# A hybrid diffusion step: five half tiles of the dense experts stay in PSUM, one bank rotates, and the finish is reordered

## The chip, the cores and the metric

One core of one Trainium2 chip runs the whole kernel. The metric is the device time of an execution in microseconds; the median of several is what is compared.

## The reference, cut to what matters

One layer for 256 context tokens and 1024 latent tokens, model width 1024: modulation, windowed attention and RG-LRU into one output projection, then PEER, which picks 16 of 16384 experts for each of 8 heads and each token, and a last norm. The change touches the end of the first half and PEER:

```python
o_att = attend(q, k, v, attn_sink)
o_rnn, hf, hb = rglru_mixer(xr, yg, rg_w_a, rg_b_a, rg_w_i, rg_b_i, rg_lambda, h0_f, h0_b)
mix = jnp.concatenate([o_att, o_rnn.astype(o_att.dtype)], axis=-1)
x = x + ga1 * jnp.einsum('bsm,md->bsd', mix, w_out)
h2 = modulated_norm(x, g_ffn, sh2, sc2)
x = x + ga2 * peer(h2, pq, psk, pu, pv)
...
u = jnp.take(u_tab, eid, axis=0)
act = jax.nn.gelu(jnp.einsum('td,thkd->thk', xb, u).astype(jnp.float32))
vv = jnp.take(v_tab, eid, axis=0)
return jnp.einsum('thk,thkd->td', (g * act).astype(vv.dtype), vv)
```

## The kernel before

Tokens go in tiles of 128: two context tiles and eight latent tiles. The stages run in this order: modulation, the context tiles' first half, latent projection and recurrence (lproj), latent attention (lattend), the latent finish (fin), retrieval of the expert numbers (ret, `choose`), `spread` with the early experts, and `dense`.

PEER is done in two ways. Six latent tiles are **dense**: each of the 16384 experts is applied to them, in 128 steps of 128 experts. A step multiplies the expert rows `u` with the tiles' activations (48 matmuls of 384 columns, in `experts_in`), applies gelu, multiplies with the tokens' expert weights (`gt`) and adds the product with the rows `v` to the tiles' sums. 44 of the 128 steps have their first part done earlier, in the stage early, and fetch it from DRAM (`ad`). The two context tiles and the last two latent tiles are **gathered** (`mix`): for each of 128 picks a row of `u` and a row of `v` come by an indirect DMA from GpSimd's queue (L859, L873), and VectorE forms one dot product (L862) or one scaled sum (L879). That is 4 x 256 = 1024 gathers. They are written between other work: `tick` adds a mark's microseconds to a count and lets the next gather out whenever the count reaches the step of the stage; the gathers of dense are also ordered behind the instruction that marked them (`paced`).

Products are made as three matmuls of split operands (`mm3`, L138 to L140): a high and a low part of each side.

In `dense`, experts go in rounds of two (`GROUP`). `add` makes a round's products: six tiles of two halves of 512 columns, 12 halves, each the sum of 6 matmuls. `N_RES` tiles (two, so four halves, `res`) keep their sums in PSUM over all rounds. The other eight halves rotate through two banks (`rot`): ScalarE evicts each to `q` (L764), and VectorE adds it to `acc` in SBUF (L765). The resident products are written first, then the rotating ones.

`finish` for the latent tiles does, tile by tile, 32 matmuls of the output projection (two halves, L526), two VectorE steps a half (L528, L529), the squares (L535), rstd on VectorE and GpSimd (`rstd_of`, L145 to L151), the scaling (L537), eight transposes with their copies (`to_columns`, L248, L255), a split (L134, L135), for the gathered tiles another set of transposes (L545), and at last a mark of 14 us. `final` makes the last norm of a tile and stores it.

The instructions of all engines come from a compiler that orders each engine's queue by priority (the written order) and by what is ready in its own model; so an instruction can stand ahead of one written before it, unless a dependence forbids it.

## Time and profile before

| | us |
|---|---|
| median of 3 runs | 3565.87 |
| lowest and highest | 3563.97, 3566.43 |
| the profiled execution | 3568.34 |
| its span, first to last instruction | 3566.5 |
| TensorE busy in the span | 3210.4 |
| VectorE busy | 3111.0 |
| GpSimd busy | 1716.4 |
| ScalarE busy | 1429.9 |

Busy times are of that one execution. PE is TensorE's matmuls, PEld its weight loads, DVE is VectorE, ACT is ScalarE, POOL is GpSimd, SP is the queue of most DMAs. A matmul's duration in the timeline runs to a modelled end, so products that follow each other closely overlap: the distance of two starts is what one costs. PEclk is the granted clock of TensorE, 1.00 being 2.4 GHz. A wait is put down to the releaser that came last.

### The profile page before, as it was taken

How to read it: one execution, taken by the hardware profiler on the slowest of the kernel's cores; microseconds unless marked ns; L12 is line 12 of the kernel's file. 1: busy time of each engine (PE TensorE's matmuls, PEld its weight loads, DVE VectorE, ACT ScalarE, POOL GpSimd, SP SyncE). 2: the span in 40 equal slices, each digit the busy share in tenths (PEclk: the TensorE clock that was granted, in tenths of full speed). 3: DMA queues.
4: the chain of work that ended last, by engine and by line, in shares of the span. 5: the costliest groups of instructions: out<-in, count | busy, mean ns of one | idle time of the engine just before them, and what ended most of it. 6: DMA issues, size and time to landing. Idle time of an engine off the chain costs nothing.

```text
span 3566.5 us, 48580 instructions
## 1 busy us (share of the span) xinstructions
PE 3210.4 (90%) x16982; PEld 2704.1 (76%) x16982; DVE 3111.0 (87%) x6762; ACT 1429.9 (40%) x2242; POOL 1716.4 (48%) x1146
## 2 busy tenths in 40 slices
PE   7788868777999888888899999999999999999994
PEld 4477645433889877778788888878888887888884
DVE  4649989877999999993599999989999998999998
ACT  5734647523112344433333334333334333333432
POOL 0012451466521223443266666656666655666665
PEclk9799989988999999999999999999999999999997
DMA  8342652588621367795699999989999998999996
GB/s 331 136 152 82 216 206 83 185 276 290 219 89 31 122 199 214 233 315 185 242 325 337 337 330 334 340 308 335 329 328 339 327 340 290 332 327 336 335 339 223
DMA packets 349141, 918.19 MB, mean 257 GB/s; under 512 B 29144, under 2 KB 150104, under 8 KB 345824
## 3 DMA queue, kind: packets, MB, share of 16 engines
q0 software_dynamic: 147456, 536.94, 42.9%
q1 hardware_dynamic: 201440, 378.16, 30.8%
q8 instruction: 133, 2.18, 0.2%
q14 instruction: 112, 0.92, 0.1%
HBM read 834.48 MB, written 80.50 MB: 257 GB/s over the span
## 4 chain that ended last, share of the span: by engine, by line
PE 43%; DVE 22%; issue 8%; DMA 8%; POOL 3%; ACT 2%; SPq 0%; POOLq 0%; DVEq 0%; ACTq 0%
PE u L138 6%; PE u L140 6%; PE u L139 6%; PE rot L138 5%; PE rot L140 5%; PE rot L139 5%; DVE acc L879 3%; DVE row L862 3%; DMA row<-in_peer_u,eid 2%; PE res L138 2%; PE res L139 2%; PE res L140 2%; DMA row<-in_peer_v,eid 2%; DMA ad<-a 2%; DVE oh L699 1%
## 5 line engine op out<-in xcount | busy, mean ns | idle before, releaser
L859 POOL DMA_INDIRECT row<-in_peer_u,eid x512 | 749.9, 1465 | 603.3 <-DVE acc L879 201.7
L873 POOL DMA_INDIRECT row<-in_peer_v,eid x512 | 719.9, 1406 | 583.6 <-DVE acc L879 283.7
L138 PE MATMUL u<-hh,uh 128*128 128x384 f32 x2048 | 707.1, 345 | 22.4 <-ACT a L1028 22.4
L140 PE MATMUL u<-hh,ul 128*128 128x384 f32 x2048 | 705.6, 345 | 4.7 <-DVE ul L135 4.7
L139 PE MATMUL u<-hl,uh 128*128 128x384 f32 x2048 | 707.1, 345 | 0.0
L879 DVE SCALAR_TENSOR_TENSOR acc<-row,w,acc 128x1024 f32<-128x1024 f32 x508 | 663.4, 1306 | 25.2 <-DMA row<-in_peer_v,eid 23.7
L862 DVE SCALAR_TENSOR_TENSOR row<-row,h 128x1024 f32<-128x1024 f32 x512 | 623.0, 1232 | 62.8 <-DMA row<-in_peer_u,eid 62.6
L764 ACT ACTIVATE q<-rot 128x512 f32<-128x512 f32 x504 | 300.0, 597 | 523.5 <-PE rot L140 295.5
L138 PE MATMUL rot<-vh,ah 128*128 128x512 f32 x1024 | 409.1, 400 | 16.6 <-ACT q L764 16.1
L138 PEld LDWEIGHTS u<-hh,uh 128*128 128x128 f32 x2048 | 394.7, 193 | 29.8 <-ACT a L1028 23.8
L140 PEld LDWEIGHTS u<-hh,ul 128*128 128x128 f32 x2048 | 394.2, 192 | 9.7 <-DVE ul L135 5.1
L139 PE MATMUL rot<-vl,ah 128*128 128x512 f32 x1024 | 401.4, 392 | 0.0
L140 PE MATMUL rot<-vh,al 128*128 128x512 f32 x1024 | 400.6, 392 | 0.0
L139 PEld LDWEIGHTS u<-hl,uh 128*128 128x128 f32 x2048 | 394.6, 193 | 4.5
L765 DVE TENSOR_TENSOR acc<-q,acc 128x512 f32<-128x512 f32 x504 | 341.8, 686 | 45.4 <-ACT q L764 42.3
L140 PE MATMUL mm<-hh,wl 128*128 128x256 f32 (+2 forms) x848 | 289.7, 342 | 9.8 <-POOL wl L135 6.9
L138 PE MATMUL mm<-hh,wh 128*128 128x256 f32 (+2 forms) x848 | 286.3, 338 | 5.6 <-ACT wh L134 5.6
L139 PE MATMUL mm<-hl,wh 128*128 128x256 f32 (+2 forms) x848 | 284.3, 335 | 0.0
L134 ACT ACTIVATE uh<-u 128x1024 fp32r<-128x1024 f32 x128 | 135.8, 1061 | 331.3 <-PE u L139 302.0
L135 POOL TENSOR_TENSOR ul<-u,uh 128x1024 fp32r<-128x1024 f32 x44 | 122.8, 2791 | 277.8 <-ACT uh L134 237.5
L138 PEld LDWEIGHTS rot<-vh,ah 128*128 128x128 f32 x1024 | 193.4, 189 | 74.9 <-ACT q L764 36.7
L140 PEld LDWEIGHTS rot<-vh,al 128*128 128x128 f32 x1024 | 193.2, 189 | 41.5
(271 smaller groups left out, 5955.3 us busy)
## 6 DMA issues: line engine op xcount, KB each, us to landing
u<-in_ut SPq DMA_DIRECT2D x128, 512.0 KB
v<-in_peer_v SPq DMA_DIRECT2D x128, 512.0 KB
gd<-stg SPq DMA_DIRECT2D x12, 4096.0 KB
gt<-gd SPq DMA_DIRECT2D x64, 768.0 KB
w<-in_w_mod SPq DMA_DIRECT2D x24, 1024.0 KB
ad<-a SPq DMA_DIRECT2D x88, 192.0 KB
a<-ad SPq DMA_DIRECT2D x44, 384.0 KB
w<-in_w_query SPq DMA_DIRECT2D x32, 512.0 KB
```

The costliest lines, as they stand in the source:

```text
L134: A.activation(hi, src, AF.Copy)
L135: return (eng or V).tensor_tensor(lo, src, hi, op=OP.subtract)
L138: T.matmul(out, lhs[0], rhs[0], start=first, stop=False)
L139: T.matmul(out, lhs[0], rhs[1], start=False, stop=False)
L140: T.matmul(out, lhs[1], rhs[0], start=False, stop=last)
L699: V.tensor_tensor(oh.rearrange(four, j=2), o2.rearrange(four, j=2), pairs(gh, ts), op=OP.mult)
L764: A.activation(q, p, AF.Copy)
L765: tick(share / (2 * (N_DENSE - N_RES)), V.tensor_tensor(y, q, y, op=OP.add))
L859: G.indirect_dma_start(out=u, out_offset=None, in_=i["peer_u"], in_offset=bass.IndirectOffsetOnAxis(ap=eid[:, k:k + 1], axis=0))
L862: V.scalar_tensor_tensor(u, u, 1.0, h2, op0=OP.mult, op1=OP.mult, accum_out=act[:, j:j + 1])
L873: G.indirect_dma_start(out=v, out_offset=None, in_=i["peer_v"], in_offset=bass.IndirectOffsetOnAxis(ap=eid[:, k:k + 1], axis=0))
L879: V.scalar_tensor_tensor(acc, v, w[:, j:j + 1], acc, op0=OP.mult, op1=OP.add)
```

## The change

Four things change.

- `dense`: `N_RES` counts halves now, five of them, in five banks; one bank rotates in place of two. `add` writes one rotating product, then one resident product, and so on; after five such pairs the last two rotating products follow each other. Seven halves a round are evicted and added. In the tail, `final` takes tile 2's first half from PSUM and its second from `acc`.
- `D_STEP` goes from 2.05 to 2.0: a gather for every 2.0 us of marks in dense.
- `finish` of the latent tiles: the norm of a tile (`normed`) is written after the next tile's matmuls, its transposes are queued behind the last of them (`issue_after`), and the marks are 3 after each half and 2 after a tile in place of 14. `x` has three buffers, `f` two.
- `final`: one multiplication in place of two runs on GpSimd.

```diff
-N_RES = 2
+N_RES = 5
-D_STEP = 2.05
+D_STEP = 2.0
@@ finish
+        def normed(t, x, behind):
+            ss = wk.tile([P, 1], F32, name="ss", bufs=2)
+            f = wk.tile([P, KD, P], F32, name="f", bufs=2)
+            A.activation(f.rearrange("p k t -> p (k t)"), x, AF.Square, accum_out=ss)
+            rs = rstd_of(ss, wk)
+            A.activation(x, x, AF.Copy, scale=rs)
+            hh, hl, us = dest(t)
+            with tc.issue_after(behind) if behind else nullcontext():
+                to_columns(ps, f, x, hh, hl, us, a2, b2, cond)
...
+        waiting = None
...
-                    x = wk.tile([P, D], F32, name="x", bufs=2)
+                    x = wk.tile([P, D], F32, name="x", bufs=3 if lat else 2)
...
-                        T.matmul(p, oT, wo[c0][:, k, wc], start=(k == 0), stop=(k == KD - 1))
+                        ins = T.matmul(p, oT, wo[c0][:, k, wc], start=(k == 0), stop=(k == KD - 1))
...
+                    if lat:
+                        tick(3)
...
-                to_columns(ps, f, x, hh, hl, us, a2, b2, cond)
...
-                tick(14)
+                if not lat:
+                    normed(t, x, None)
+                    tick(14)
+                    continue
+                if waiting:
+                    normed(*waiting, ins.ins)
+                waiting = t, x
+                tick(2)
+        if waiting:
+            normed(*waiting, None)
@@ dense
-            res = [[ps.tile([P, 512], F32, name=f"res{x}{hf}") for hf in range(2)] for x in range(N_RES)]
+            res = [ps.tile([P, 512], F32, name=f"res{r}") for r in range(N_RES)]
-            acc = [st.tile([P, D], F32, name=f"acc{x}") for x in range(N_RES, N_DENSE)]
+            acc = {x: st.tile([P, D], F32, name=f"acc{x}") for x in range(N_RES // 2, N_DENSE)}
@@ add
-                for it in group:
-                    for x in range(N_RES):
-                        for hf in range(2):
-                            product(res[x][hf], x, hf, it, 0, P - 1)
-                for x in range(N_RES, N_DENSE):
-                    for hf in range(2):
-                        p = ps.tile([P, 512], F32, name="rot", bufs=2)
+                stay = iter(range(N_RES))
+                for r in range(N_RES, 2 * N_DENSE):
+                    x, hf = divmod(r, 2)
+                    p = ps.tile([P, 512], F32, name="rot")
+                    for it in group:
+                        product(p, x, hf, it, c0, c0 + GROUP - 1)
+                    y = acc[x][:, hf * 512:(hf + 1) * 512]
+                    if c0 == 0:
+                        A.activation(y, p, AF.Copy)
+                    else:
+                        q = wk.tile([P, 512], F32, name="q", bufs=2)
+                        A.activation(q, p, AF.Copy)
+                        tick(share / (2 * N_DENSE - N_RES), V.tensor_tensor(y, q, y, op=OP.add))
+                    for s in stay:
                         for it in group:
-                            product(p, x, hf, it, c0, c0 + GROUP - 1)
...
+                            product(res[s], *divmod(s, 2), it, 0, P - 1)
+                        break
@@ final
-        (G if N_CTX + N_RES <= t < N_CTX + N_DENSE and t % 2 == 0 else V).tensor_tensor(y, y, ga2, op=OP.mult)
+        (G if N_CTX + N_RES // 2 < t < N_CTX + N_DENSE and t % 2 == 0 else V).tensor_tensor(y, y, ga2, op=OP.mult)
```

## Rows read from the trace of the kernel before

**Rows 1.** The page's totals: busy us (share of span) x instructions.
```profile
PE 3210.4 (90%) x16982; PEld 2704.1 (76%) x16982; DVE 3111.0 (87%) x6762; ACT 1429.9 (40%) x2242; POOL 1716.4 (48%) x1146
```
**Rows 2.** Busy us by stage: PE, PEld, DVE, ACT, POOL; then clock, DMA share, GB/s.
```profile
706.00:888.00 182.00, 134.22 (x348) 65.70 (x348) 132.88 (x198) 54.60 (x105) 115.64 (x90) 0.86 0.84 282
...
1420.00:1640.00 220.00, 187.48 (x1466) 168.09 (x1465) 205.58 (x441) 86.87 (x108) 89.06 (x50) 0.94 0.87 274
1640.00:1720.00 80.00, 67.84 (x360) 65.70 (x361) 15.83 (x48) 20.34 (x29) 16.62 (x9) 0.90 0.47 160
1720.00:3521.00 1801.00, 1774.69 (x8617) 1565.08 (x8615) 1679.20 (x2158) 687.38 (x1043) 1138.97 (x770) 0.99 0.90 326
3521.00:3566.50 45.50, 0.38 (x2) 0.00 (x0) 39.44 (x57) 11.04 (x20) 15.65 (x10) 0.55 0.39 149
```
**Rows 3.** Timeline of TensorE in dense: start us, us, engine, line, operation.
```profile
1902.57 0.39 PE L138 MATMUL rot<-vh,ah 128*128 128x512 f32 x1
1913.45 0.34 PE L138 MATMUL u<-hh,uh 128*128 128x384 f32 x1
1930.10 0.39 PE L138 MATMUL res<-vh,ah 128*128 128x512 f32 x1
```
**Rows 4.** Timeline of the finish: TensorE, and one row of ScalarE.
```profile
761.95 1.10 PE L248 MATMUL tr<-ident,x 128*128 128x128 f32 x8 [1.90 <-ACT x L537]
...
768.90 3.60 PE L526 MATMUL mm<-w,gy 128*128 128x512 f32 x8
772.33 3.60 PE L526 MATMUL mm<-w,qT 128*128 128x512 f32 x8
773.72 1.06 ACT L535 ACTIVATE f<-x 128x1024 f32<-128x1024 f32 x1 [7.07 <-DVE x L529]
781.52 1.97 PE L248 MATMUL tr<-ident,x 128*128 128x128 f32 x8 [5.59 <-ACT x L537]
...
880.03 1.97 PE L248 MATMUL tr<-ident,x 128*128 128x128 f32 x8 [17.89 <-ACT x L537]
```
**Rows 5.** Waits in the finish: us in total, times, longest us.
```profile
PE tr L248 <- ACT x L537: 46.2, 8, 17.9
```
**Rows 6.** Groups of VectorE in the finish; the last by min/median/max ns.
```profile
L862 DVE SCALAR_TENSOR_TENSOR row<-row,h 128x1024 f32<-128x1024 f32 x43 | 54.3, 1268 | 28.2 <-DMA row<-in_peer_u,eid 28.0
L879 DVE SCALAR_TENSOR_TENSOR acc<-row,w,acc 128x1024 f32<-128x1024 f32 x38 | 48.8, 1284 | 16.2 <-DMA row<-in_peer_v,eid 15.6
...
L528 DVE TENSOR_TENSOR y<-mm,ga x16: 678/682/692, 719.0 to 866.0; 128x512 f32<-128x512 f32 x16
```
**Rows 7.** Gathers issued ahead of the finish: ns min/median/max, first and last start.
```profile
L859 POOL DMA_INDIRECT row<-in_peer_u,eid x48: 937/1149/2744, 364.6 to 670.9; - x48
L873 POOL DMA_INDIRECT row<-in_peer_v,eid x46: 937/1000/2816, 404.1 to 703.8; - x46
```
**Rows 8.** Busy time of the finish's matmuls alone up to 862; columns as rows 2.
```profile
706.00:862.00 156.00, 116.73 (x256) 0.90 0.83 279
```
**Rows 9.** Timeline in dense: a product's last matmul and its eviction.
```profile
1903.71 0.39 PE L140 MATMUL rot<-vh,al 128*128 128x512 f32 x1
...
1904.13 0.60 ACT L764 ACTIVATE q<-rot 128x512 f32<-128x512 f32 x1 [2.94 <-PE rot L140]
```
**Rows 10.** The page's costliest groups: busy us, mean ns, idle before.
```profile
L765 DVE TENSOR_TENSOR acc<-q,acc 128x512 f32<-128x512 f32 x504 | 341.8, 686 | 45.4 <-ACT q L764 42.3
```
**Rows 11.** Waits of TensorE in dense, columns as rows 5.
```profile
PE rot L138 <- ACT q L764: 10.7, 7, 3.3
```
**Rows 12.** Timeline of TensorE in a round without expert products.
```profile
1958.82 0.39 PE L138 MATMUL rot<-vh,ah 128*128 128x512 f32 x1
1959.05 0.39 PE L138 MATMUL res<-vh,ah 128*128 128x512 f32 x1
```
**Rows 13.** Timeline of the tail.
```profile
3528.11 3.40 DVE L837 TENSOR_TENSOR row<-row,vh 128x1024 f32<-128x1024 f32 x1 [0.77 <-DMA vh<-modd]
```
**Rows 14.** Busy time in one stretch of dense, columns as rows 2.
```profile
2900.00:3000.00 100.00, 89.76 (x406) 78.29 (x405) 88.62 (x114) 33.17 (x51) 62.42 (x43) 0.93 0.90 324
```

## What the change was predicted to do

> **What bounds the kernel now.** I read the page's engine totals first, then the busy time by stage, then in the two stages that the change touches the timeline and the waits. The totals [rows 1] show TensorE busy 90% and VectorE 87% of the span: neither can be judged without the stages. The stages [rows 2] are, in us from the span's start: the finish of the latent tiles 706 to 888; retrieval, spread and the early experts 888 to 1720 (its last two stretches stand there); dense 1720 to 3521; the tail to 3566.5.
>
> In **dense** TensorE is the bound. Its products start every 0.227 us without a gap: 48 rot products from 1902.57 to 1913.45, and 96 expert products (u, 384 columns) in the 16.65 us from 1913.45 to 1930.10 [rows 3]. A round of two experts has 72 products of the first kind (16.3 us); 42 of the 64 rounds also have 96 of the second, and 22 have theirs from the early stage. So 42 x 33.0 + 22 x 16.3 = 1744 us of the 1801 in dense are columns that must pass; only 57 us are start, waits and end. VectorE is busy 1679 of the 1801 us, close behind.
>
> In the **finish** nothing is full: TensorE is busy 134 of 182 us at a granted clock of 0.86 (a mix of its two levels, 1.2 and 2.4 GHz), VectorE 133. One tile's four groups of eight matmuls take 4 x 3.43 = 13.7 us at the full clock (768.90 to 772.33 [rows 4]), so eight need 110. TensorE then waits ahead of the transposes of x: 5.59 us in the row at 781.52, 17.89 us in that at 880.03 (the last tile), 46.2 us over the eight tiles [rows 4, 5]. Those transposes stand inside the next tile's matmuls, and what they wait for is a chain (squares, rstd on VectorE and GpSimd, scaling) whose VectorE steps queue behind gathers: 81 gathered rows are worked off in the stretch, ten a tile, with 28.0 + 15.6 us of waiting for rows to land [rows 6].
>
> **The gathers are handed out by marks.** A mark adds its microseconds to a count, and each 1.9 (finish), 4.0 (retrieval), 1.0 (early) or D_STEP (dense) emits one. Counted by the source: attention (64 x 0.6 + 38 x 1.3)/1.9 = 46, finish 8 x 14/1.9 = 59, retrieval 16 x 8 x 1.7/4.0 = 54, early 90: 249 ahead of dense, and 1024 - 249 = 775 left. But the compiler doesn't hold to the written order: 48 + 46 gathers are issued by 706 [rows 7], where the marks allow 46. So gathers slip ahead into idle time, and at the finish nearly all of its own have been done already; those in it belong to later stages.
>
> **The change, part by part.**
>
> *Finish, order of transposes.* Each tile's norm is now written after the next tile's matmuls, and its transposes are queued behind them. The cover is that tile's 13.7 us of matmuls. The chain from x to the transposes took 8 us in a tile that I followed (squares from 773.72, transposes from 781.52 [rows 4]), and x stands two steps of 0.69 and perhaps one gather of 1.28 behind the last matmul [rows 6]: 11 us, under the cover by some 3. Up to 862 the floor is 110 us of matmuls and, for seven tiles, 1.1 us of transposes each (row at 761.95 [rows 4]), 117.5 us, where the trace has 156: 38.5 us can come back, part of it as clock (0.90 there [rows 8]). The last tile has no cover and keeps its 26 us to 888, perhaps 5 less.
>
> *Finish, marks.* 3 + 3 + 2 in place of 14 a tile: 8 x 8/1.9 = 33 gathers in place of 59. VectorE's own work per tile is near 5 us (four steps of 0.69 [rows 6], a split about as long as a gather's step, the short rstd steps), so 13.7 + 1.1 us leave room for seven gathers at 1.28. Fewer stand ahead of a tile's chain, but those that slip in from retrieval still do. I take 38.5 + 5 less 7.5 for them: **36 us less**. Bounds: 10 (ten gathers a tile as now, 182/81 = 2.2 us each, and only waits on the order go) and 50.
>
> *From 888 to 1720.* The 26 gathers leave VectorE, but from 1640 to 1720 it is idle 64 of 80 us while TensorE works off the early experts [rows 2]. TensorE's work is unchanged, and it is busy 187 of 220 and 68 of 80 us there. So the stage only starts earlier: 0.
>
> *Dense, fewer sums.* Seven halves rotate in place of eight: 63 of 504 sums at 0.686 us on VectorE and as many evictions at 0.60 on ScalarE go [rows 9, 10], 43 us of VectorE. Against it stand 26 gathers (20 in dense, six behind it), 26 x 1.28 = 33 us. VectorE gains 10 us in all, on an engine that isn't the bound; of the 10.7 us that rot products wait for evictions [rows 11] I take 2 off.
>
> *Dense, one bank.* Rot and resident products now alternate: rot0, res0, ... rot4, res4, rot5, rot6. After each of the first five, 6 products (1.36 us) hide the eviction, the same distance as the second bank gave. Rot5 to rot6 has no such cover. By the rows, a rot's last product starts at 1903.71, its eviction at 1904.13, and that ends at 1904.73; the next product would have been due at 1903.94 [rows 9]: 0.79 us a round, **51 us** if it lies bare 64 times. Behind it wait rot6 and then the next expert's products. The other end is nothing: the compiler fills TensorE's queue by readiness, as when it starts a rot product at 1958.82 and then goes back to resident ones at 1959.05 [rows 12], and u products of the next expert are ready. I take 4, near the row that shows the filling. Also moved: nothing on the queues of SP or GpSimd but the 26 gathers' issue. The part together: **+2**.
>
> *Pace and end.* Marks in dense add up to 64 x 8 + 42 x 25 + 21 x 1.4 = 1591 us (the first round's sums carry none): 776 gathers at 2.05, enough for 775, so the last tile's final stage lies among the products. At 2.0 there are 795 for 801: six gathers and that tile's final stage come behind dense. Six at 1.28 are 7.7 us on a VectorE that is busy 39 of 45.5 us in the tail [rows 2], and a last chain of norm and store that others covered before adds a few. A gain: one multiplication moves from GpSimd to VectorE, where one took 3.40 us while GpSimd ran its own [rows 13]. **+10**, between 0 and +20.
>
> *Sum:* -36 + 2 + 10 = -24. The profiled run took 3568.3 (span 3566.5 and 1.8 around it), 2.5 above the median of 3565.9; against the median, **3542**.
>
> **The rivals.**
> A. The gap of the one bank lies bare. For it: the model that orders the queue has other durations than the chip. Against it: rows 12, and only 10.7 us of such waits in 1700 us today. 3565.9 - 36 + 51 - 2 + 10 = 3589, slower. It decides from about 34 us of gap, some 0.5 us a round: there the gain is gone.
> B. The finish hardly shortens, because gathers of retrieval fill whatever its marks leave. For it: rows 7. 3565.9 - 10 + 2 + 10 = 3568, no change.
> C. All works: finish 50 less, dense 6 less as sums and evictions are spread out, the six gathers slip into idle time (+2): 3512.
> D. The short gaps also cost clock. In 2900 to 3000 TensorE lost 10 us in few waits and its clock shows 0.93; over all of dense it is 0.99 [rows 2, 14]. If each gap had the six products of rot6 at the lower level, 1.36 us more 64 times, 87 us come on top of A's: 3676. The Trainium skill (TensorE: Matmul & The Clock Gate, A second HAM failure mode: psum-queue depth-cycling) speaks against this change here: it tells of a kernel that cycled through PSUM banks and whose short idle times between groups made the clock swing between its levels. The trace bears that out only for longer waits so far, and by that rule alone the time would be D's.
>
> **How the numbers follow.** Forecast 0.54 (its own range 3524 to 3558), A 0.14 (with partial gaps from 3560), B 0.14, C 0.15, D 0.03. The likeliest is 3542. The range 3512 to 3586 leaves out half of C, D and the full gap. By the bound of 0.2% (7 us, about what a measurement of this kernel can tell from no change): faster 0.50 of the forecast and C, 0.65; the same 0.04 of it, 0.11 of B and 0.02 of A, 0.17; slower 0.12 of A, 0.03 of B and D, 0.18.
>
> **What would show it.** Right: the finish ends near 850 with transposes behind full tiles of matmuls and few waits on x; dense keeps products 0.227 us apart, with u products between rot5 and rot6; 441 evictions and 441 sums; six gathers behind the last product. Wrong: a wait of rot on the eviction in most of 64 rounds (A), ten gathers a tile still in the finish (B), a clock under 0.95 in dense (D). The forecast falls above all if the compiler orders the finish otherwise than it is written.

## The result, and the profile after

The changed kernel takes **3668.7 us** (median of 3 runs, 3667.3 to 3669.7) against 3565.9: ratio **1.029**, 95% interval 1.027 to 1.031. It is slower by 103 us where 24 less were forecast. The profiled execution took 3669.7 (span 3668.0).

The page's totals after, which answer [rows 1]:

```profile
PE 3259.0 (89%) x16982; PEld 2700.9 (74%) x16982; DVE 3077.3 (84%) x6700; ACT 1399.4 (38%) x2182; POOL 1662.3 (45%) x1145
```

TensorE is busy 49 us more with the same 16982 matmuls. Busy time by stage, which answers [rows 2] (columns as there): finish, retrieval to dense (and its last 80 us once more), dense, tail.

```profile
735.00:919.00 184.00, 131.47 (x339) 62.55 (x336) 138.49 (x198) 54.28 (x106) 119.88 (x94) 0.88 0.86 292
919.00:1736.00 817.00, 727.90 (x5077) 673.24 (x5075) 668.26 (x2869) 281.04 (x377) 194.14 (x96) 0.96 0.50 151
1640.00:1720.00 80.00, 77.64 (x437) 77.00 (x436) 0.00 (x0) 17.26 (x27) 21.55 (x9) 0.98 0.34 108
1736.00:3614.00 1878.00, 1819.50 (x8639) 1566.53 (x8640) 1679.58 (x2142) 657.22 (x986) 1121.69 (x791) 0.99 0.89 320
3614.00:3668.00 54.00, 0.55 (x3) 0.12 (x1) 43.79 (x61) 10.71 (x19) 19.34 (x14) 0.54 0.43 154
```

Read against before, from edge to edge (first product of dense 1712.2 before, 1736.2 after):
- The **finish** is 184 us long where it was 180, and it begins 30 us later: the last attention product stands at 735, before at 705. The loss is older than the finish.
- Retrieval to dense takes 817 us (827 before); VectorE does nothing at all in the 80 us of the third row.
- **Dense** is 1878 us (1809): 37 us more of busy TensorE and 32 more of idle.
- The **tail** is 54 us (45.5). That term was forecast at +10.

So 24 us are lost ahead of dense, 69 in it and 8 behind it: 101 in the two spans, 3566.5 and 3668.0.

### The profile page after: what moved, and what is told of

It reads as the page before. It is cut to its first block, busy times and chain, and to the rows that moved or that the text cites. A ratio compares the mean times of both kernels' runs of the same rounds, so it can differ in the third digit from the quotient of the medians.

```text
span 3668.0 us, 48444 instructions
## 1 busy us (share of the span) xinstructions
PE 3259.0 (89%) x16982; PEld 2700.9 (74%) x16982; DVE 3077.3 (84%) x6700; ACT 1399.4 (38%) x2182; POOL 1662.3 (45%) x1145
## 4 chain that ended last, share of the span: by engine, by line
PE 40%; DVE 25%; issue 13%; DMA 12%; POOL 6%; ACT 3%; SPq 0%; POOLq 0%; DVEq 0%; ACTq 0%
PE u L138 5%; PE u L139 5%; PE u L140 5%; DMA row<-in_peer_u,eid 4%; PE rot L138 4%; PE rot L140 3%; PE rot L139 3%; DMA row<-in_peer_v,eid 3%; DVE acc L897 3%; DVE row L880 3%; POOL row L891 3%; POOL row L877 2%; PE res L138 2%; PE res L139 2%; PE res L140 2%
## 5 line engine op out<-in xcount | busy, mean ns | idle before, releaser
L877 POOL DMA_INDIRECT row<-in_peer_u,eid x512 | 720.6, 1407 | 651.5 <-DVE row L880 228.8
L891 POOL DMA_INDIRECT row<-in_peer_v,eid x512 | 707.8, 1382 | 514.7 <-DVE acc L897 262.3
L140 PE MATMUL u<-hh,ul 128*128 128x384 f32 x2048 | 702.1, 343 | 6.3 <-POOL ul L135 4.5
L780 ACT ACTIVATE q<-rot 128x512 f32<-128x512 f32 x441 | 262.8, 596 | 630.2 <-PE rot L140 407.8
L138 PE MATMUL rot<-vh,ah 128*128 128x512 f32 x896 | 374.5, 418 | 65.9 <-ACT ah L134 36.6
L140 PEld LDWEIGHTS u<-hh,ul 128*128 128x128 f32 x2048 | 390.5, 191 | 14.9 <-POOL ul L135 6.1
L140 PE MATMUL rot<-vh,al 128*128 128x512 f32 x896 | 354.7, 396 | 1.1 <-DVE al L135 1.1
L139 PE MATMUL rot<-vl,ah 128*128 128x512 f32 x896 | 353.7, 395 | 0.0
L781 DVE TENSOR_TENSOR acc<-q,acc 128x512 f32<-128x512 f32 x441 | 300.4, 685 | 21.6 <-ACT q L780 20.8
L138 PEld LDWEIGHTS rot<-vh,ah 128*128 128x128 f32 x896 | 169.4, 189 | 154.5 <-ACT q L780 84.9
L135 DVE TENSOR_TENSOR vl<-v,vh 128x1024 fp32r<-128x1024 f32 x128 | 154.7, 1219 | 125.2 <-DMA gt<-gd 119.0
L138 PE MATMUL res<-vh,ah 128*128 128x512 f32 x640 | 253.4, 397 | 0.0
```

Of the source, the lines that this page charges most:

```text
L135: return (eng or V).tensor_tensor(lo, src, hi, op=OP.subtract)
L138: T.matmul(out, lhs[0], rhs[0], start=first, stop=False)
L139: T.matmul(out, lhs[0], rhs[1], start=False, stop=False)
L140: T.matmul(out, lhs[1], rhs[0], start=False, stop=last)
L780: A.activation(q, p, AF.Copy)
L781: tick(share / (2 * N_DENSE - N_RES), V.tensor_tensor(y, q, y, op=OP.add))
```

## The experiments

Seventeen kernels ran; their numbers are the order in which they ran. "Before" beside them had medians of 3561 to 3565 us. Each median rests on 4 to 10 runs (11 and 12: a single one) and its ratio is known to between 0.1% and 0.4% (4 to 13 us) either way. A single profile of one kernel can stand up to 12 us off its median, so small differences are taken from the medians.

### The two halves alone

**Experiment 1** puts the new `finish` into the kernel before, **experiment 2** the new `dense` (with N_RES 5 and `final`'s condition); both keep D_STEP 2.05.

> The kernel before with the new finish alone (order of the transposes, marks 3 + 3 + 2, three x and two f buffers); dense, the resident tiles and D_STEP 2.05 as before. Theory 1 (two separate losses: some 24 us ahead of dense from the new finish, some 69 us in dense from the one rotating bank): 3590 us, first dense load near 1727 where it was near 1703, dense some 1818 long. Theory 2 (gathers are the common cause: the finish hands out fewer, dense has more to do and its queue of rows is late): dense grows here too, by 40 us or more, and the time is 3630 or above. Theory 3 (the finish gains as predicted and only dense loses): 3530 to 3545.

Measured: **3631.4** (1.019, 1.017 to 1.021). Dense begins at 1728 and is 1808 us long, as before. The other 51 us stand where none of the theories had them, in a tail of 96 us. The groups of gathers on VectorE behind the last product, of experiment 1, then of before (count | busy, mean ns | idle time ahead of them, and what ended it):

```profile
L896 DVE SCALAR_TENSOR_TENSOR acc<-row,w,acc 128x1024 f32<-128x1024 f32 x17 | 21.9, 1286 | 11.6 <-DMA row<-in_peer_v,eid 11.3
L879 DVE SCALAR_TENSOR_TENSOR row<-row,h 128x1024 f32<-128x1024 f32 x16 | 21.3, 1350 | 3.9 <-DMA row<-in_peer_u,eid 3.9
```
```profile
L879 DVE SCALAR_TENSOR_TENSOR acc<-row,w,acc 128x1024 f32<-128x1024 f32 x7 | 11.0, 1574 | 0.0
```

33 gathers against 7: the 26 that the new marks took out of the finish.

> The kernel before with the new dense stage alone (five resident halves, seven rotating halves through one bank, products alternating); finish and D_STEP 2.05 as before. Theory 1 (one bank): the start of dense unchanged near 1703, dense some 69 us longer, 3635 us, with waits of rot on its eviction and of PE on activations as in the changed kernel. Theory 2 (gathers): dense within 20 us of before, 3566 to 3585. Theory 3: 3635 as well; it differs from theory 1 in the first kernel.

Measured: **3583.5** (1.007, 1.004 to 1.009): +20, not +69, within theory 2's range; dense 1826 us, tail 44. So the losses of the halves are +68 and +20 at a D_STEP of 2.05. The changed kernel at that pace takes 3688.3 (experiment 7 below), so beside the new finish the new dense costs 57 us, 37 more than alone. The parts don't simply add up.

### The second f buffer

The new finish gives `f`, the normed columns, two buffers, and the context finish, which runs the same function some 500 us earlier, gets them too. **Experiment 5** is the kernel before with that alone:

```diff
-                f = wk.tile([P, KD, P], F32, name="f")
+                f = wk.tile([P, KD, P], F32, name="f", bufs=2)
```

> The kernel before with two buffers in place of one for f, the normed columns in the finish, and nothing else. The context finish has the same line, ahead of the latent projections. Theory 1 (this buffer alone lets the compiler write the latent projections in another order, and that is the 20 us which are lost ahead of attention): the first score product starts near 555 where it started near 533, the time is 3580 to 3590. Rival (the order of the transposes or the marks of the latent finish reach back that far): first score product at 533, 3560 to 3570.

Measured: **3589.4** (1.007, 1.005 to 1.009), theory 1. The first score product, with its wait, of before, of experiment 5 and of the changed kernel (timeline: start us, us, instruction, [idle before, releaser]):

```profile
533.89 0.58 PE L431 MATMUL s<-kh,qs 128*128 128x256 f32 x1 [20.73 <-DVE qs L414]
```
```profile
554.91 0.58 PE L431 MATMUL s<-kh,qs 128*128 128x256 f32 x1 [24.51 <-DVE qs L414]
```
```profile
559.11 0.58 PE L431 MATMUL s<-kh,qs 128*128 128x256 f32 x1 [25.25 <-DVE qs L414]
```

One buffer makes 21 of the 25 us that are lost by here. The context finish itself ends 5 us sooner (its last transposes at 230.3, at 235.6 in experiment 2, whose code is that of before up to there). But with `f` free sooner, VectorE's instructions stand in another order at the seam to the latent projections: the splits `hl` and `wl` ahead of the convolution's `xc`, where they stood among and behind them. In that stage TensorE's gate products (`g`) now wait 12.1 us for `xc`, before 2.9 (waits from 330 to 500, of before and of experiment 5: us in total, times, longest):

```profile
PE g L358 <- DVE xc L346: 2.9, 3, 1.3
```
```profile
PE g L358 <- DVE xc L346: 12.1, 3, 6.0
```

That is 9 of the 21 us. The same products wait 9.8 us for `av` in place of 4.9, the wait ahead of the first score product is 3.8 longer, and the granted clock from 330 to 500 is 0.92 in place of 0.98. That the buffer costs this time is measured; how the new order leads to each wait isn't shown.

### The marks

**Experiment 6** is experiment 1 with the old marks:

```diff
-                    if lat:
-                        tick(3)
...
-                tick(2)
+                tick(14)
```

> The first experiment with the marks of the finish as before: 14 behind each tile, none behind its halves; the order of the transposes and the buffers are the new ones. Theory 1 (the 26 gathers which the new marks take out of the finish are what stands behind dense): the tail is near 45 us instead of 96, the stretch up to dense stays some 20 us late, 3580 to 3590. Rival (the new order itself defers the gathers): tail near 90, 3625 to 3635.

Measured: **3587.4** (1.007, 1.004 to 1.009), tail 44.7. As theory 1 had it: the marks cost **44 us** (3631.4 - 3587.4). What did they buy? In experiment 1 VectorE works off 83 gathers in the 180 us of the finish, in experiment 6 it is 84. The finish didn't get any emptier, since gathers of retrieval were drawn forward, and dense begins within 4 us of the same time (1727.7, 1731.8). Retrieval to dense lost the 26 (33 gathers, 59 in experiment 6). VectorE's hole ahead of dense isn't new with the marks: from 1640 to 1700 it is idle in experiment 6 too, and all but idle in experiment 5 (0.7 us busy). The marks make it longer: from 1600 to 1640 VectorE is busy 4.5 us, 36.3 in experiment 6.

### The order of the transposes

**Experiment 14** is experiment 6 with one f buffer in the context, so it has only the new order with its buffers in the latent finish (the third `x`, the second `f`):

```diff
-            f = wk.tile([P, KD, P], F32, name="f", bufs=2)
+            f = wk.tile([P, KD, P], F32, name="f", bufs=2 if lat else 1)
```

> The kernel before with only the new order of the transposes and the third x buffer in the latent finish; marks, f in the context, dense and D_STEP as before. Theory 1 (the finish is as long as its gathers on VectorE, whatever order TensorE has): 3555 to 3568. Rival (the order is worth the predicted time once f and marks are out of the way): 3525 to 3545.

Measured: **3555.3** (0.998, 0.997 to 0.999), at theory 1's lower end: 8 us faster than before, and the fastest kernel of all that ran. Its gain is a quarter of the forecast. TensorE's last group of latent matmuls, the last tile's transposes and the first expert product (timeline, as above), and under them the last matmuls and the first expert product of before:

```profile
843.86 3.60 PE L547 MATMUL mm<-w,gy 128*128 128x512 f32 x8
...
872.04 1.97 PE L248 MATMUL tr<-ident,x 128*128 128x128 f32 x8 [17.20 <-ACT x L517]
...
876.92 0.67 PE L138 MATMUL u<-hh,uh 128*128 128x384 f32 x1
```
```profile
860.68 1.02 PE L526 MATMUL mm<-w,gy 128*128 128x512 f32 x2
...
884.91 0.67 PE L138 MATMUL u<-hh,uh 128*128 128x384 f32 x1
```

From the last attention product (702.1, before 705.4) to the end of the last matmul are 145.4 us, before 156.3: TensorE does run ahead by 10.9. Then it waits: from there to the first expert product 29.5 us, before 23.2. VectorE's chain to the last tile's transposes is hardly further: they start 170.0 us behind the last attention product, before 174.7 (880.03 in [rows 4]).

**Experiments 11 and 12** let the gathers into the queue only behind the finish, in the old order and in the new one (12 with the new marks, which find an empty queue there):

```diff
-        queue.extend(mix(t) for t in range(N_CTX))
...
         for _ in fin:
             pass
+        queue.extend(mix(t) for t in range(N_CTX))
```

> The kernel before with the gathers let into the queue only behind the finish, so that none can stand in attention or in the finish; they come later, so the whole time is longer by some 100 us or more and says nothing here. Asked is the stretch from the last attention product to the last latent matmul and to the first expert product, 156 and 180 us before. Theory 1 (gathers on VectorE are what delays the chain to the transposes): near 125 and 145. Rival (the order of the transposes is what costs): within 10 us of before.

> The new finish (one f buffer in the context) with the gathers let in only behind it, dense as before; compared with the run beside it. Theory 1 (without gathers the chain is short in either order): within 8 us of the old order. Rival (the order is worth what was predicted once no gathers stand in the way): near 118 us up to the last latent matmul, 15 us or more under the old order.

Measured from the last attention product to the end of the last matmul and to the first expert product: 152.3 and 163.5 us in the old order, 139.7 and 155.6 in the new. Both expectations missed, because the finish was not bare: 54 gathers stand in it in both kernels (experiment 12's groups; columns as above), though every one is written behind it (and 90 ahead of it, as in before).

```profile
L879 DVE SCALAR_TENSOR_TENSOR row<-row,h 128x1024 f32<-128x1024 f32 x32 | 39.0, 1222 | 13.2 <-DMA row<-in_peer_u,eid 12.9
L896 DVE SCALAR_TENSOR_TENSOR acc<-row,w,acc 128x1024 f32<-128x1024 f32 x22 | 28.2, 1283 | 14.6 <-DMA row<-in_peer_v,eid 14.5
```

This is the plainest proof of what the marks can't do: the place where a gather is written doesn't hold it. With some 28 gathers fewer the old finish is 16 us shorter up to the first expert product (179.5 in before) and the new one 19 (174.9 in experiment 14), while the order is worth 5 us with all the gathers and 8 with the fewer. So it follows the gathers more than the order. Whether their steps on VectorE or the transfers of their rows make that time, these runs don't separate: the DMA engines' busy share up to the first expert product is 0.69 and 0.72 in 11 and 12, and 0.84 and 0.87 in before and experiment 14.

### Dense: one bank, the alternation, and what stands beside them

**Experiment 4** alternates the products as the change does, but with four resident and eight rotating halves through two banks (and `final`'s condition as before). **Experiment 9** is experiment 2 with the resident products spread over all six gaps. The edits, each against experiment 2:

```diff
-N_RES = 5
+N_RES = 4
-                    p = ps.tile([P, 512], F32, name="rot")
+                    p = ps.tile([P, 512], F32, name="rot", bufs=2)
```
```diff
-                stay = iter(range(N_RES))
+                stay = iter([(s, it) for s in range(N_RES) for it in group])
...
-                    for s in stay:
-                        for it in group:
-                            product(res[s], *divmod(s, 2), it, 0, P - 1)
-                        break
+                    for s, it in islice(stay, 2 if r < N_RES + 4 else 1):
+                        product(res[s], *divmod(s, 2), it, 0, P - 1)
```

> The kernel before with the products of dense written alternately as in the change, but four resident halves and eight rotating ones through two banks as before. Theory 1 (the one bank is what costs): 3560 to 3575. Theory 1b (the alternating order costs, since it puts resident products where a rot's next half would have gone and moves the sums): 3600 to 3640 with two banks also. Theory 2 (gathers): 3560 to 3575.

Measured: **3578.8** (1.004, 1.002 to 1.006), dense 1829: 15 us are lost with two banks too. That is below the range of 1b, yet no part of theory 1: the alternation costs by itself.

> The second experiment (new dense alone, 2.05) with its resident products spread over all six gaps between the rotating halves, 2, 2, 2, 2, 1 and 1 units of three products, so that three products (0.68 us) stand between the last two halves too. Theory 1 (the 20 us of the second experiment are the uncovered gap of the one bank, some 0.3 us in a round with expert products and up to 0.8 without): 3565 to 3575, no expert products between the last two halves, short gaps about as many as before. Rival (the alternating order costs through later activations and sums, as with two banks in the fourth experiment): 3578 to 3590.

Measured: **3597.5** (1.009, 1.006 to 1.012). It is above both ranges, and theory 1 falls as put. But the cover didn't come to stand where it was written: in the trace a round goes rot, res 4, rot, res 2, then two u products, then the last rot with a step of 0.34 in place of 0.23. So the experiment doesn't say what a covered gap would be worth.

**Experiments 10, 13 and 15** look for the rest: 10 is the changed kernel with the edits of experiments 6 and 14 and D_STEP 2.05; 13 is 10 with the new marks; 15 is experiment 2 with the edit of experiment 5.

```diff
-D_STEP = 2.0
+D_STEP = 2.05
```

> The changed kernel with three of its edits taken back: marks of the finish 14 behind each tile, one f buffer in the context finish (two in the latent one), D_STEP 2.05. What is left is the order of the transposes, the third x buffer and the new dense. Theory 1 (the extra cost of the new dense in company of the new finish comes with the 26 gathers that are left for dense, the start is late by the f buffer alone): first score product near 533, dense near 1826, tail near 45, 3575 to 3590. Rival (the new order of the finish makes the new dense dear by itself): dense near 1865, 3615 or above.

Measured: **3580.9** (1.004, 1.002 to 1.006), dense 1834, tail 45: theory 1. Against experiment 14 the new dense costs 26 us here.

> The tenth experiment (one f buffer in the context, D_STEP 2.05, new order and new dense) with the new marks of the finish, 3 + 3 + 2: the changed kernel with f and D_STEP alone taken back. Theory 1 (parts add up once f is taken away; the new dense is dear in company of the late start that f makes): 3581 and the 44 us of the marks, 3620 to 3632, dense near 1830, tail near 95. Rival (the new marks shift the gathers against the rounds, and that makes the new dense dear): 3650 to 3670, dense 1855 or more.

Measured: **3653.8** (1.026, 1.023 to 1.029): the rival. Tail 94 (+49), and dense 1866 (+32).

> The second experiment (new dense alone, 2.05) with two f buffers. Theory 1 (the new dense is dear in company of the late start that f makes): 3583 and 25 and most of the 37 us that are open, 3630 to 3645. Rival (the marks do that): 3600 to 3612, dense near 1828.

Measured: **3609.9** (1.013, 1.010 to 1.017), the rival's range: f and the new dense add up (25 + 20). What doesn't add up is the new **marks** beside the new dense: 73 us, where they cost 44 beside the old. (The two pairs differ in f as well, but f costs 25 to 34 us in each of four pairs: 5 against before, 6 against 14, 15 against 2, 7 against 13.) It isn't the number of gathers either: in dense 770 are worked off in experiment 13 and 771 in 10, and yet it is 32 us longer.

**How dense waits.** Experiment 2's round at 2020 shows the one bank. TensorE: the last product of rot5, first and last of the four u products that the compiler put behind it, then rot6; and ScalarE's eviction of rot5:

```profile
2021.63 0.39 PE L140 MATMUL rot<-vh,al 128*128 128x512 f32 x1
2021.86 0.34 PE L138 MATMUL u<-hh,uh 128*128 128x384 f32 x1
...
2022.38 0.33 PE L138 MATMUL u<-hh,uh 128*128 128x384 f32 x1
2022.71 0.50 PE L138 MATMUL rot<-vh,ah 128*128 128x512 f32 x1
2023.04 0.39 PE L139 MATMUL rot<-vl,ah 128*128 128x512 f32 x1
```
```profile
2022.06 0.60 ACT L763 ACTIVATE q<-rot 128x512 f32<-128x512 f32 x1 [2.12 <-PE rot L140]
```

The gap is filled here, as forecast, yet not to its end: rot6 starts 0.33 us after a u product (0.17 otherwise), and its second product 0.33 after its first (0.23): 0.26 us instead of 0.79. But it isn't once a round: such a gap of four u products between two rotating halves stands 96 times in experiment 2's dense, 0.27 us each (the median), 26 us in all, since the compiler places resident products elsewhere in some rounds. And there is more than that. Waits on dense, of before, of experiment 2 and of the changed kernel, from the first product to the last (PEld is TensorE's weight load, which waits a little ahead of the product):

```profile
PEld rot L138 <- ACT q L764: 36.7, 66, 5.3
...
PE res L138 <- ACT ah L134: 14.9, 3, 10.5
DVE a L784 <- DMA a<-ad: 7.0, 5, 2.4
```
```profile
PEld rot L138 <- ACT q L763: 65.7, 179, 4.4
DVE a L787 <- DMA a<-ad: 31.3, 16, 4.6
...
PE rot L138 <- ACT ah L134: 16.5, 4, 10.5
```
```profile
PEld rot L138 <- ACT q L780: 84.9, 206, 5.2
...
DVE a L804 <- DMA a<-ad: 38.7, 15, 4.3
PE rot L138 <- ACT ah L134: 36.6, 13, 10.3
```

Two things grow, by the number of waits. Waits on the eviction: from 66 to 179 with one bank alone (37 in experiment 4 with two). And waits of a product on the activations `ah`: 3 in before, 4 in experiment 2, 13 in the changed kernel. VectorE's waits for the early experts' `a` from DRAM grow as well, with two banks too (29.9 us in experiment 4, 7.0 in before); what they cost isn't shown. Sorted by the distance of each product's start from the last one's, from 1780 to 3500 (number, us above the 0.227 and 0.173 of undisturbed products):

| kernel | short, under 0.5 us | long | at the lower clock |
|---|---|---|---|
| before | 116, 15 | 10, 22 | 53, 9 |
| experiment 4 (two banks) | 80, 13 | 18, 39 | 72, 13 |
| experiment 2 (one bank) | 223, 29 | 10, 21 | 26, 5 |
| experiment 13 (and new marks) | 268, 34 | 22, 45 | 60, 11 |
| changed kernel | 251, 34 | 28, 57 | 57, 11 |

The one bank costs by short waits; the marks (and the alternation with two banks) by long ones. What a long one is, the changed kernel shows at 3071, on VectorE, ScalarE and TensorE:

```profile
3070.07 1.22 DVE L135 TENSOR_TENSOR vl<-v,vh 128x1024 fp32r<-128x1024 f32 x1
3074.93 1.23 DVE L880 SCALAR_TENSOR_TENSOR row<-row,h 128x1024 f32<-128x1024 f32 x1 [3.64 <-DMA row<-in_peer_u,eid]
...
3076.08 0.95 DVE L804 TENSOR_TENSOR a<-a,gt 128x768 f32<-128x768 f32 x1
```
```profile
3077.07 0.84 ACT L134 ACTIVATE ah<-a 128x768 fp32r<-128x768 f32 x1 [7.98 <-DVE a L804]
```
```profile
3073.02 0.40 PE L140 MATMUL rot<-vh,al 128*128 128x512 f32 x1
3077.96 0.79 PE L138 MATMUL rot<-vh,ah 128*128 128x512 f32 x1 [4.55 <-ACT ah L134]
...
3081.83 0.63 PE L140 MATMUL res<-vh,al 128*128 128x512 f32 x1
3082.25 0.48 PE L138 MATMUL rot<-vh,ah 128*128 128x512 f32 x1
3082.57 0.40 PE L139 MATMUL rot<-vl,ah 128*128 128x512 f32 x1
```

A gathered row lands 3.64 us late; VectorE stands still ahead of it, though the step behind it, the second expert's `a`, needs no row. ScalarE splits `a` late, and TensorE waits at the first rotating half after the three products of the first expert. In the old order a round begins with the first expert's products on all four resident halves: 12 products, 2.7 us, that need no second expert. As written, the same lateness is covered there by 2.7 us and here by 0.7. (In about a third of the rounds the compiler itself puts 12 to 15 resident products of the first expert ahead.) With the marks equal, experiment 1 (old order) waits 24.1 us for `ah` and experiment 13 (new order) 38.3. That the new marks raise these waits in both orders is measured (15.2 in experiment 6 to 24.1, and 18.7 in experiment 10 to 38.3); why, is not: that they shift the gathers against the rounds is argued only. What makes the rows late is open as well: the DMA engines' busy share in dense is 0.90 before and 0.89 after, and no run separates them from the order of the queues.

### The pace

**Experiment 3** is the kernel before with D_STEP 2.0, **experiment 8** experiment 1 with it, **experiment 7** the changed kernel with 2.05:

```diff
-D_STEP = 2.05
+D_STEP = 2.0
```

> The kernel before with D_STEP 2.0 in place of 2.05, and nothing else. Theory 1: dense within 10 us of before, tail shorter or equal, 3560 to 3575. Theory 2 (a faster pace makes VectorE wait for rows that have not landed, and TensorE for the activations behind them): 3580 to 3610, with VectorE's waits on landing rows in dense doubled.

Measured: **3580.4** (1.005, 1.004 to 1.007), at theory 2's lower end: dense 1830, tail 36. VectorE's waits for rows in dense went from 20.5 to 38.2 us, near the doubling of theory 2. Dense is 21 us longer with only five gathers more in it (774, 769 before), so the pace itself costs.

> The first experiment with D_STEP 2.0, or the changed kernel with the dense stage of before. Theory 1 (the parts add up): some 20 us more in dense than the first experiment and some 45 us less behind it, near 3610; the new dense's share of the change is then near 55. Theory 2 (pace on top of more gathers in dense is what makes it long): dense near 1860 here too, 3640 to 3660.

Measured: **3631.3** (1.017, 1.013 to 1.021): dense 1832 (+24 on experiment 1), tail 61 (-35), and no gain in all. Seventeen gathers more stand in dense, and it is 23.5 us longer. That would be 1.4 us each, near a step of VectorE (1.22 to 1.28), but experiment 3 pays 21 us for five at the same pace: number and pace aren't separated here.

> The changed kernel with D_STEP 2.05 in place of 2.0. Theory 1 (the parts add up): the first experiment's 3631 and the 20 us of the new dense alone, 3645 to 3660, with some 31 gathers in a tail near 100 us and dense near 1828. Theory 2 (the faster pace on top of the new order is what makes dense 1878 long): dense 1805 to 1815, 3630 to 3640. Rival (the new dense costs its 70 us in company of the new finish at any pace): dense near 1875, over 3700.

Measured: **3688.3** (1.035, 1.032 to 1.037): dense 1866, tail 94. Here the faster pace of the change is worth 20 us, since it shortens a tail of 94; but the new dense costs 57 beside these marks (3688.3 - 3631.4), between theory 1 and the rival.

### Gathers where VectorE idles

**Experiments 16 and 17** add to experiment 14 more gathers behind the early experts and take them from dense; 16 as below, 17 with 110.0 and 2.1.

```diff
-D_STEP = 2.05
+D_STEP = 2.15
...
-AFTER = 90.0
+AFTER = 130.0
```

> The fourteenth experiment (the new order of the transposes alone) with 40 more gathers handed out at the end of the early experts (AFTER 130 in place of 90) and 40 fewer in dense (D_STEP 2.15 in place of 2.05). It tests what a gather costs by its place, the other way round from the new marks: those took gathers from a stage that holds them and left them to the end. Theory 1 (VectorE is idle for most of the 80 us ahead of dense, so gathers there cost nothing, and each one less behind TensorE's products saves its VectorE time where it is late): 3525 to 3550, VectorE busy over 45 of the 80 us ahead of dense. Rival (dense is bound by TensorE and gathers there are free at the old pace; those handed out early only run into the head of dense): 3553 to 3575.

> The same at half the size: 20 more gathers behind the early experts (AFTER 110) and 20 fewer in dense (D_STEP 2.1). Theory 1: half the gain of the run beside it, 3540 to 3553. Rival: within 7 us of 3555, or the loss of the run beside it halved.

Measured: **3588.3** (1.007, 1.004 to 1.009) and **3589.6** (1.009, 1.007 to 1.011): theory 1 and the rival fall, and the loss isn't halved with the number. Waits from 1560 to 1745, of experiment 16:

```profile
PE u L138 <- ACT a L1043: 29.5, 4, 23.7
ACT L1043 <- DMA ad<-a: 18.6, 1, 18.6
PE g L718 <- DVE oh L714: 15.9, 6, 8.0
```

VectorE was idle there, but the gathers reach back: the spread ends at 1643 (1615 in experiment 14), since its `oh` steps queue behind them, ScalarE waits 18.6 us ahead of an early expert's `a` until a store of an earlier one has landed, and TensorE 29.5 us for `a`. Dense begins at 1742 instead of 1696. Dense is no shorter either, 1808 us against 1807, though 36 gathers fewer stand in it (733, 769): those taken out gave nothing back.

## Why the prediction was wrong, point by point

The medians lay the loss out along one path, edit by edit (105 us against the 3563.7 that before took beside experiment 14):

| step | us | difference |
|---|---|---|
| before, to the order of the transposes and its buffers alone (experiment 14) | 3563.7 to 3555.3 | -8 |
| and the second f buffer in the context finish (6) | to 3587.4 | +32 |
| and the new marks (1) | to 3631.4 | +44 |
| and the new dense (7) | to 3688.3 | +57 |
| and D_STEP 2.0, the changed kernel | to 3668.7 | -20 |

The shares depend on the path: the new dense is +20 alone and +57 here, at the end.

**What bounds the finish: the reading that failed first.** The prediction found that in the finish "nothing is full". By busy time that is so. But [rows 2, 6] had the rest: VectorE's 132.9 us of work and its 28.0 + 15.6 of standing at rows that had not landed are 176 of the 182 us. It had no time left: in its rows, short steps of the norm stand behind a gather that waits. How much of that is VectorE's own bound and how much the transfers' (DMA share 0.84 in [rows 2], 0.86 after) isn't separated. After the change it is the same: 138.5 busy and 24.3 + 23.5 waiting, 186 counted in 184. VectorE's gathers from 735 to 919, after:

```profile
L897 DVE SCALAR_TENSOR_TENSOR acc<-row,w,acc 128x1024 f32<-128x1024 f32 x46 | 62.7, 1364 | 25.5 <-DMA row<-in_peer_v,eid 24.3
L880 DVE SCALAR_TENSOR_TENSOR row<-row,h 128x1024 f32<-128x1024 f32 x39 | 47.6, 1222 | 23.7 <-DMA row<-in_peer_u,eid 23.5
```

They are 85, where [rows 6] counted 81: ten a tile still, rival B's mechanism. The Trainium skill (Perfetto Trace Analysis, Identifying the Most-Contended Engine) takes occupancy as the measure for VectorE. By that rule a quarter of the finish was free on it; the trace disagrees, with 176 of 182 us spent working or at rows.

**Finish, order (-36 forecast with the marks, -8 measured).** The step that failed: "x stands two steps of 0.69 and perhaps one gather of 1.28 behind the last matmul [rows 6]: 11 us, under the cover by some 3". The timeline of VectorE for the first tile after the change, whose last matmul group began at 746.08 and ended 3.6 us later, with TensorE's transposes below it:

```profile
750.57 4.00 DVE L897 SCALAR_TENSOR_TENSOR acc<-row,w,acc 128x1024 f32<-128x1024 f32 x3
755.55 1.28 DVE L897 SCALAR_TENSOR_TENSOR acc<-row,w,acc 128x1024 f32<-128x1024 f32 x1 [0.97 <-DMA row<-in_peer_v,eid]
...
758.70 0.68 DVE L549 TENSOR_TENSOR y<-mm,ga 128x512 f32<-128x512 f32 x1
...
760.89 0.69 DVE L550 TENSOR_TENSOR x<-y,x 128x512 f32<-128x512 f32 x1
...
765.41 0.27 DVE L149 TENSOR_SCALAR rs_s<-rs_r,rs_m 128x1 f32<-128x1 f32 x1
768.77 1.28 DVE L897 SCALAR_TENSOR_TENSOR acc<-row,w,acc 128x1024 f32<-128x1024 f32 x1 [3.09 <-DMA row<-in_peer_v,eid]
...
772.42 0.17 DVE L151 TENSOR_TENSOR rs_r<-rs_r,rs_s 128x1 f32<-128x1 f32 x1
```
```profile
773.88 1.97 PE L248 MATMUL tr<-ident,x 128*128 128x128 f32 x8 [7.31 <-ACT x L517]
```

From the end of the matmuls (749.7) to the transposes are 24 us, not 11: five gathers stand ahead of `y`, and between the short steps of the norm (`rs`) stands a gather each, one of which waits 3.09 us for its row. The cover of 13.7 was sized well; what it had to cover was not. In all the transposes wait 47.4 us over eight tiles, 46.2 before [rows 5]:

```profile
PE tr L248 <- ACT x L517: 47.4, 8, 20.6
```

**Finish, marks (priced at less than nothing, +44 measured).** The count was right: 26 gathers moved to later. The prices were not. Their leaving was to empty the finish; the compiler refilled it, though the prediction itself said from [rows 7] that gathers slip ahead. Their coming was priced at "20 in dense, six behind it" with dense free: "on an engine that isn't the bound". Behind dense they cost 51.4 / 26 = 2.0 us each (experiment 1 against 6). In dense no price for one comes out of the runs: 17 more go with 23.5 us (8 against 1), five more at that pace with 21 (3 against before), 36 fewer with none (16 against 14), and beside the new dense the marks cost 32 us with the same number (13 against 10). What the runs do show is that dense wasn't free: TensorE has 26 us to spare there and VectorE is busy 93%.

**The f buffer (not priced at all, +25 alone, +32 beside the order, +34 in the changed kernel at 2.05).** The prediction said of 888 to 1720 that it "only starts earlier", and of everything ahead of 706 nothing: a second buffer of a tile in a function that an earlier stage calls too was no step of it. It had the general clause, that the forecast falls "if the compiler orders the finish otherwise than it is written"; what was ordered otherwise was the stage behind the other finish.

**Dense (+2 forecast, +20 alone, +69 in the changed profile).** The gap: bounds 0 to 51, taken at 4; the rows have it filled with some 0.27 us left over, 96 times in place of 64, 26 us; all the short waits of the table grow by 14 against before, which had others. So the mechanism was right and the term mis-sized: [rows 12] showed that the compiler fills, not that it fills to the end. The step that was missing is the alternation: it was costed only for the bank, while it also takes away the 12 products that hid a late second expert. With two banks it costs 15 us (experiment 4); 7 of them are waits for `ah` (21.8, before 14.9), the rest isn't traced.

**Tail (+10 forecast, +8.5 measured).** Right in size: 12 gathers stand behind the last product and 7 before, five more where six were counted. The count for before, none, was seven short.

**The rivals.** A (3589): its gap exists, at a third of its size and half as often again. B (3568): its mechanism is what happened in the finish, and its price was too mild by all that the marks did later. C fell. D (3676) has nearly the measured time by chance: the clock of dense is 0.99 before and after, and products at the lower level make 11 us after, 9 before. The Trainium skill (TensorE: Matmul & The Clock Gate, A second HAM failure mode: psum-queue depth-cycling) tells of a kernel whose short idle times between groups made the clock swing. This kernel has such waits, 251 of them, and its trace doesn't show the swing: the granted clock of dense is 0.99.

## What to carry to other kernels

Count an engine that works in order as having no time to spare when its busy time and its waiting at the head of its queue fill the stage; there, a better order on another engine mostly moved the wait. A piece of filler work has a price by where it lands, not by where it is written. That price doesn't follow from the length of its step: behind the last product it was 2.0 us for a step of 1.3, and in dense, nearly full on two engines, the pace and the place cost more than the number. A buffer count in a function that two stages call is an edit of both, and is priced for both.

## What the runs showed of the hardware

- After a wait of 4.55 us TensorE's products stood 0.43 us and more apart in place of 0.23, until 4.3 us after it resumed (3077.96 to 3082.25, rows above): the lower of its two levels. 251 waits under 0.5 us left the granted clock of dense at 0.99.
- One profile can't rank kernels that differ by a few tenths of a per cent: dense had its first product at 1712, 1703, 1703 and 1705 us in before and experiments 2, 3 and 4, and at 1716 in experiment 9, whose code ahead of dense is that of before.
